# The first MLP product of a decoder layer as seven block products of 256 tokens instead of eight

## The chip, the cores and the metric

The kernel runs on one core of a Trainium2 chip. The metric is the device time of one execution in microseconds (us), the median over runs; a profiled execution is one such run whose instructions were recorded, and its span runs from the first to the last recorded instruction. Engines: PE multiplies matrices (PEld is its loading of weights), DVE, ACT and POOL work elementwise, SP only issues transfers; a transfer (DMA) is issued from the queue of SP, ACT or POOL.

## What is computed

One layer of a decoder on 512 tokens of 1024 features, in float32: a normalised input is projected to gates, queries, keys, values and two short branches; attention, a gated convolution and a pooling are mixed and projected back; then an MLP. The part that matters here:

```
merged = gates[0]*(y_pool @ w_pool_up) + gates[1]*(y_conv @ w_conv_out) + gates[2]*(y_attn @ w_attn_up)
x = x + merged @ w_o                                   # 1024 x 1024
h2 = rms_norm(x, norm_mlp)
x = x + jnp.square(jax.nn.relu(h2 @ w_ff1)) @ w_ff2    # w_ff1: 1024 x 4096, w_ff2: 4096 x 1024
```

The sum of squares inside `rms_norm` is over the features of a token, so its reciprocal root can be multiplied in after `h2 @ w_ff1`, as a factor per token.

## The kernel before

Features lie on the 128 partitions, tokens along the row, so that a tile [128, 512] holds 128 features of all tokens. A weight streams in as units of [128, 1024] (512 KB) by one transfer each on SP's queue; `split` (L115 to L120) cuts it into two float32r parts, `wh` by ACT and `wl` = unit - `wh` by DVE, in buffers of which there are three of each. `mm3` (L122 to L127) makes a float32 product of three passes on PE: `wh` with the high part of the moving tile, `wh` with its low part, `wl` with its high part. One unit feeds 8 x 3 passes of 512 columns.

The order of the work on each engine is fixed when the program is built, by a scheduler that works through the written order; at run time an engine takes its instructions strictly in that order, and each waits for what it reads.

The MLP stage is preceded by the output projection: `wo_mm` (L505) multiplies two of eight merged tiles into four of the eight PSUM banks (a bank is [128, 512]) per unit. `x2_evac` (L555) then adds a bank to the residual `res[m]` (L556) and makes the two parts `xs` of the MLP's input (L164, L167). The first MLP product runs over pairs of output chunks (L581 to L597); `ff1_evac` takes a bank through relu, the factor `rstd2` and the square (L576, L577). `rs2` sums squares of `res` on POOL (`Rstd.add`, L200) and over the partitions by a product with a tile of ones (L204). The second product (L599 on) splits each of its 32 moving tiles (L405, L406) and adds into eight banks.

Of the kernel before, what the change touches and what calls it, by code (L numbers as in the profile page):

```python
# [36 lines left out]
AHEAD = 1  # units of weights split ahead of their use  # L37
WARM = 9  # products of zeros that wake the tensor engine's clock until the first data is there
# [11 lines left out]
def z_order():  # L50
    """The 128-column chunks of w_in, as (kind, index, first column), in the order of use."""
# [14 lines left out]
def hybrid_layer(ctx: ExitStack, tc: tile.TileContext, xT, wst, pmix, vecs, consts, outT):  # L66
# [5 lines left out]
    apool = ctx.enter_context(tc.tile_pool(name="apool", bufs=1))  # L72
# [11 lines left out]
    def tmp(dt=F32):  # L84
        return apool.tile([P, S], dt, tag="tmp", bufs=13, name=nm("tmp"))
# [14 lines left out]
    ahead = deque()  # L100
    rp = None
    n_loaded = [0]

# [3 lines left out]
    def unit():  # L107
        while len(ahead) <= AHEAD and n_loaded[0] < wst.shape[0]:
            raw = raw_unit()
            nc.sync.dma_start(raw, wst[n_loaded[0]])  # L110
            ahead.append(split(raw, rp if n_loaded[0] in LONG else wpool))
            n_loaded[0] += 1
        return ahead.popleft()
# [8 lines left out]
    def mm3(out, w, cols, x, start, stop):  # L122
        """out += w[:, cols].T @ x in float32: both operands split, three float32r passes."""
# [9 lines left out]
    warm = cpool.tile([P, S], BF16, name="warm")  # L133
# [18 lines left out]
    cst = cpool.tile([P, NCONST], F32, name="cst")  # L152
# [6 lines left out]
    bd = cpool.tile([P, P], F32R, name="bd")  # L159
# [10 lines left out]
    def rsqrt_start(total, n):  # L170
        """1 / sqrt(total / n + EPS): by ln and exp, and what then takes one Newton step in float32."""
# [16 lines left out]
    class Rstd:  # L188
        """1 / rms over the features, from their squares as they come in."""
# [44 lines left out]
    # Work that hangs on a chunk of z goes on in steps, one after each later chunk.  # L234
# [12 lines left out]
    at = ExitStack()  # L247
    atp = at.enter_context(tc.tile_pool(name="atp", bufs=1))
# [34 lines left out]
    def v_evac(kind, idx, b):  # L283
# [8 lines left out]
        # [values of one head | ones | values of the other]  # L292
# [101 lines left out]
        # 1 / dn by ln and exp, then one Newton step in float32; dn is at least 1  # L394
# [110 lines left out]
    def wo_mm(half, k, outs):  # L505
        if k % 2 == 0:
            wo_w[half] = unit()
        for i in range(4):
            mm3(outs[i], wo_w[half], cols(4 * (k % 2) + i), merged[k], k == 0, k == KC - 1)

    attn_w = None
    for m in range(KC):
# [10 lines left out]
        if m == 0:  # L523
# [3 lines left out]
            rp = ctx.enter_context(tc.tile_pool(name="rp", bufs=1))  # L527
            for k in range(KC):
# [23 lines left out]
    h2 = [None] * KC  # L552
    rs2 = Rstd()

    def x2_evac(m):  # L555
        nc.vector.tensor_tensor(res[m], res[m], wo_banks[m], OP.add)  # L556
        h2[m] = split_gain(res[m], vec[:, V_NF + m:V_NF + m + 1], True)

    for i in range(4, 8):
        wo_banks[i] = bank()  # L560
    for k in range(KC - 1):
        wo_mm(1, k, wo_banks[4:])
    wo_mm(0, KC - 1, wo_banks[:4])
    for m in range(4):
        x2_evac(m)
    wo_mm(1, KC - 1, wo_banks[4:])
    for m in range(4, 8):
        x2_evac(m)

# [1 line left out]
    f = []  # L571

    def ff1_evac(pair):
        for b in pair:
            t = br(F32) if len(f) < 20 else mg(F32)
            nc.vector.scalar_tensor_tensor(t, b, 0.0, rstd2, op0=OP.max, op1=OP.mult)  # L576
            nc.scalar.activation(t, t, AF.Square)  # L577
            f.append(t)

    done = []  # L580
    for j in range(0, NFF, 2):  # L581
        pair = [bank(), bank()]
        w2 = [unit(), unit()]
        for ks in ([range(4)] + [range(k, k + 1) for k in range(4, KC)] if j == 0 else [range(KC)]):
            for b, w in zip(pair, w2):
                for k in ks:
                    mm3(b, w, cols(k), h2[k], k == 0, k == KC - 1)
        done.append(pair)
        if j == 0:
            for t in res:  # L590
                rs2.add(t)
        if j >= 2:
            if j == 2:
                rstd2 = rs2.end("rstd2")
            for pair in done:
# [109 lines left out]
```

## Time and profile before

| | us |
|---|---|
| median of 3 runs | 824.1 (822.91 to 825.32) |
| span of the profiled execution | 822.6 |
| PE busy | 807.4 (98%) |
| loading of weights (PEld) busy | 662.4 (81%) |
| DVE busy | 424.2 (52%) |
| ACT busy | 297.7 (36%) |
| POOL busy | 63.2 (8%) |

The execution's own time was not recorded beside its span; the median of the runs lies 1.5 us above the span, which is what lies around it. PE is busy almost without a break, and its passes overlap: a pass counts as busy until its last result is out, while the next one has started. How fast PE works is therefore read from the distance between the starts of two passes, not from their durations.

### The profile page before, as it was taken

Reading aid. Unit: us, or ns where it says so; the run is one execution under the profiler, and the core shown is the slowest. Engines: PE = TensorE matmul, PEld = TensorE weight load, DVE = VectorE, ACT = ScalarE, POOL = GpSimd, SP = SyncE. Lnnn points to the kernel's source line nnn. Section 1 sums busy time; section 2 is a strip of 40 time slices with the busy share of each in tenths; the row PEclk is TensorE's granted clock in tenths of the full one; section 3 lists DMA queues with packets and bytes.
Section 4 is the critical chain, followed back from the end, with each engine's and each line's share of the span. In section 5 each row is a group of like instructions: output and inputs, shape, how many; then the busy total and the mean of one; then the engine's idle time right before and its main releaser. Section 6 shows DMA issues by size and latency. Waiting matters only on the chain. (4 is left out here: it accounts for less than half of the span.)

```text
span 822.6 us, 9086 instructions
## 1 busy us (share of the span) xinstructions
PE 807.4 (98%) x3649; PEld 662.4 (81%) x3649; DVE 424.2 (52%) x530; ACT 297.7 (36%) x398; POOL 63.2 (8%) x50
## 2 busy tenths in 40 slices
PE   7999998999999999999999999999999999999998
PEld 4888787887888888888888778888888888888886
DVE  7659686786885434554343756333333333333323
ACT  5466255742363223322232527233223332233210
POOL 6020012124200000000000320000000000000000
PEclk9999999999999999999999999999999999999999
DMA  6422221221254222222222222222222232222312
GB/s 226 154 78 82 97 77 52 90 103 52 77 166 142 100 79 103 103 102 89 91 102 77 73 106 103 96 85 102 103 103 88 91 103 102 99 83 101 102 52 102
DMA packets 24810, 80.99 MB, mean 98 GB/s; under 512 B 2880, under 2 KB 3136, under 8 KB 24768
## 3 DMA queue, kind: packets, MB, share of 16 engines
q1 hardware_dynamic: 23472, 78.19, 27.3%
q10 hardware_dynamic: 1296, 2.23, 0.9%
q8 instruction: 28, 0.46, 0.2%
q14 instruction: 14, 0.11, 0.0%
HBM read 78.31 MB, written 2.10 MB: 98 GB/s over the span
## 5 line engine op out<-in xcount | busy, mean ns | idle before, releaser
L118 ACT ACTIVATE wh<-raw 128x1024 fp32r<-128x1024 f32 x136 | 144.0, 1060 | 406.6 <-issue 212.4
L127 PE MATMUL bank<-xs,wl 128*128 128x512 f32 x720 | 280.7, 390 | 3.6 <-DVE wl L220 2.4
L125 PE MATMUL bank<-xs,wh 128*128 128x512 f32 x720 | 282.0, 393 | 1.8 <-ACT tmp L196 1.8
L126 PE MATMUL bank<-xs,wh 128*128 128x512 f32 x720 | 280.9, 390 | 2.3 <-DVE xs L167 2.2
L119 DVE TENSOR_TENSOR wl<-raw,wh 128x1024 fp32r<-128x1024 f32 x136 | 170.1, 1252 | 68.5 <-ACT wh L118 64.0
L127 PEld LDWEIGHTS bank<-xs,wl 128*128 128x128 f32 x720 | 135.2, 188 | 33.2 <-DVE wl L220 3.4
L126 PEld LDWEIGHTS bank<-xs,wh 128*128 128x128 f32 x720 | 135.2, 188 | 32.9 <-DVE xs L167 4.8
L125 PEld LDWEIGHTS bank<-xs,wh 128*128 128x128 f32 x720 | 135.1, 188 | 31.8 <-ACT tmp L196 2.7
L126 PE MATMUL bank<-tmp,wh 128*128 128x512 f32 x256 | 99.6, 389 | 0.0
L125 PE MATMUL bank<-tmp,wh 128*128 128x512 f32 x256 | 99.6, 389 | 0.0
L127 PE MATMUL bank<-tmp,wl 128*128 128x512 f32 x256 | 99.6, 390 | 0.0
L127 PEld LDWEIGHTS bank<-tmp,wl 128*128 128x128 f32 x256 | 48.0, 188 | 10.2 <-DVE wl L119 0.3
L126 PEld LDWEIGHTS bank<-tmp,wh 128*128 128x128 f32 x256 | 48.1, 188 | 10.0
L125 PEld LDWEIGHTS bank<-tmp,wh 128*128 128x128 f32 x256 | 48.1, 188 | 9.9
L518 DVE TENSOR_TENSOR tmp<-bank,rstd 128x512 f32<-128x512 f32 x24 | 16.6, 692 | 65.5 <-PE bank L127 65.4
L200 POOL TENSOR_TENSOR tmp<-tmp,tmp 128x512 f32<-128x512 f32 x14 | 23.6, 1688 | 247.7 <-ACT tmp L196 246.8
L406 DVE TENSOR_TENSOR tmp<-br,tmp 128x512 fp32r<-128x512 f32 x20 | 13.6, 690 | 44.4 <-PE bank L126 44.4
L576 DVE SCALAR_TENSOR_TENSOR br<-bank,rstd 128x512 f32<-128x512 f32 x20 | 13.5, 689 | 42.9 <-PE bank L127 42.8
L125 PE MATMUL bank<-br,wh 128*128 128x512 f32 x80 | 31.1, 389 | 0.0
L127 PE MATMUL bank<-br,wl 128*128 128x512 f32 x80 | 31.1, 389 | 0.0
L126 PE MATMUL bank<-br,wh 128*128 128x512 f32 x80 | 31.1, 389 | 0.0
L543 DVE TENSOR_TENSOR tmp<-tmp,bank 128x512 f32<-128x512 f32 x24 | 16.5, 688 | 26.0 <-PE bank L127 26.0
(129 smaller groups left out, 671.1 us busy)
## 6 DMA issues: line engine op xcount, KB each, us to landing
raw<-wst SPq DMA_DIRECT2D x136, 512.0 KB, 3.2
raw<-wst SPq DMA_DIRECT2D x8, 256.0 KB, 5.0
mg<-xT SPq DMA_DIRECT2D x8, 256.0 KB, 5.1
res<-xT ACTq DMA_DIRECT2D x8, 256.0 KB, 4.7
outT<-res SPq DMA_DIRECT2D x7, 256.0 KB, 2.0
cst<-consts SPq DMA_DIRECT2D x1, 416.0 KB, 5.4
raw<-pmix SPq DMA_DIRECT2D x1, 256.0 KB, 2.5
outT<-res SPq DMA_DIRECT2D x1, 128.0 KB, 1.8
```

The lines of the kernel that those rows point to most:

```text
L118: nc.scalar.activation(hi, raw, AF.Copy)
L119: nc.vector.tensor_tensor(lo, raw, hi.bitcast(F32), OP.subtract)
L125: nc.tensor.matmul(out, wh[:, cols], xh, start=start, stop=False)
L126: nc.tensor.matmul(out, wh[:, cols], xl, start=False, stop=False)
L127: nc.tensor.matmul(out, wl[:, cols], xh, start=False, stop=stop)
L200: nc.gpsimd.tensor_tensor(self.acc, self.acc, sq, OP.add)
L406: nc.vector.tensor_tensor(lo, t, hi.bitcast(F32), OP.subtract)
L518: nc.vector.tensor_tensor(t, b, rstd, OP.mult)
L543: nc.vector.tensor_tensor(t, t, b, OP.mult)
L576: nc.vector.scalar_tensor_tensor(t, b, 0.0, rstd2, op0=OP.max, op1=OP.mult)
```

## The change

The first MLP product is cut into 2 x 2 blocks (feature halves by column halves of a group of 512 columns of `w_ff1`, and token halves), and the eight block products of a group are replaced by seven, of sums and differences of blocks: P1, P2, Q3, Q4, Q5, Q6, Q7. Each has 8 x 3 passes of 256 columns; there are eight groups. The sums of the moving blocks (`s1` to `s4`, `n22`) are made once by DVE and ACT. The sums of the weight blocks are made by transfers: a block is loaded by SP, split, and after that a transfer on POOL's queue adds the next block onto it in place (`accum_op=OP.add`). So one tile `wx` serves P1, Q5, Q6 and Q4 in turn, with an adding transfer between each two, and one tile `wy` serves Q3 and Q7. The results are put together in `q.f` by DVE and ACT. The second half of the output projection goes by chunks (`wo_chunk`): one bank after the other, all eight merged tiles into it. Pools are placed on the right side of SBUF, so that those of the MLP take the room of the earlier ones tile by tile. Comments were removed.

```diff
+    def wo_chunk(m):
...
+        for k in range(KC):
+            mm3(wo_banks[m], w, cols(k), merged[k], k == 0, k == KC - 1)
...
+    wo_chunk(4)
+    wo_chunk(5)
+    wo_chunk(6)
+    wo_chunk(7)
+    front.close()
...
+    def w1_forms():
+        chain, row = {}, {}
+        for g in range(NFF // 4 + 1):
+            go = g < NFF // 4
+            if go:
+                x = fpool.tile([P, 1024], F32, tag="wx", bufs=3, name=nm("wx"))
+                nc.sync.dma_start(x, w1_block(g, B11))
+                yield "P1", x
+                nc.gpsimd.dma_start(x, w1_block(g, B12), accum_op=OP.add)
+            if g:
+                yield "Q7", row
+            if go:
+                yield "Q5", x
+                nc.gpsimd.dma_start(x, w1_block(g, B22), accum_op=OP.add)
+                z = raw_unit()
+                nc.sync.dma_start(z, w1_block(g, B21))
+                yield "P2", z
+                yield "Q6", x
+                nc.gpsimd.dma_start(x, w1_block(g, B21), accum_op=OP.add)
+            if g:
+                yield "Q4", chain
+            if go:
+                y = fpool.tile([P, 1024], F32, tag="wy", bufs=2, name=nm("wy"))
+                nc.sync.dma_start(y, w1_block(g, B22))
+                yield "Q3", y
+                nc.gpsimd.dma_start(y, w1_block(g, B12), accum_op=OP.add)
+                chain, row = x, y
+
+    forms = w1_forms()
+    ready = deque()
+
+    def w_fill(n):
+        while len(ready) < n:
+            nxt = next(forms, None)
+            if nxt is None:
+                break
+            ready.append((nxt[0], split(nxt[1], wpool)))
+
+    def w_form(kind):
+        w_fill(FORMS_AHEAD + 1)
+        k, w = ready.popleft()
+        assert k == kind, (k, kind)
+        return w
+
...
+    def x2_evac(m):
+        nc.vector.tensor_tensor(res[m], res[m], wo_banks[m], OP.add)
+        nc.scalar.activation(hs[m // 4][:, m % 4], res[m], AF.Copy, scale=vec[:, V_NF + m:V_NF + m + 1])
+
+    a11, a21 = hs[0][:, :, :H], hs[0][:, :, H:]
+    a12, a22 = hs[1][:, :, :H], hs[1][:, :, H:]
...
+    split_form("P1", a11, ALL)
+    w_fill(1)
+    x2_evac(4)
+    x2_evac(5)
+    ks = slice(0, 2)
+    diff(s1, a21, a22, ks)
+    split_form("Q5", s1, ks)
+    split_form("P2", a12, ks)
+    diff(s2, a11, s1, ks)
+    split_form("Q6", s2, ks)
+    for m in range(6):
+        rs2.add(res[m])
+    x2_evac(6)
+    x2_evac(7)
+    ks2 = slice(2, 4)
+    diff(s1, a21, a22, ks2)
+    split_form("Q5", s1, ks2)
+    w_fill(2)
+    split_form("P2", a12, ks2)
+    diff(s2, a11, s1, ks2)
...
+    def product(kind, out, start, stop):
+
+        (wh, wl), (xh, xl) = w_form(kind), sx[kind]
+        for b in range(2):
+            for k in range(4):
...
+                nc.tensor.matmul(o, wh[:, w], xh[:, k], start=first, stop=False, skip_group_check=True)
+                nc.tensor.matmul(o, wh[:, w], xl[:, k], start=False, stop=False, skip_group_check=True)
+                nc.tensor.matmul(o, wl[:, w], xh[:, k], start=False, stop=last, skip_group_check=True)
...
+    for g in range(NFF // 4 + 1):
+        q = None
+        if g < NFF // 4:
+            q = Group()
+            q.A = bank()
+            product("P1", q.A, True, True)
+            q.x1 = tmp()
+            nc.scalar.activation(q.x1, q.A, AF.Copy)
...
+            product("Q7", prev.R, False, True)
+            nc.vector.tensor_tensor(prev.v1, prev.R, prev.x1, OP.subtract)
+            nc.vector.tensor_tensor(prev.f[:, 2:4, H:], halves(prev.v1), halves(prev.x5), OP.add)
...
+            product("Q5", q.T, True, True)
...
+            product("P2", q.A, False, True)
...
+            product("Q6", q.R, True, True)
...
+            product("Q4", prev.R, False, True)
...
+            product("Q3", q.T, False, True)
+            nc.vector.tensor_tensor(q.f[:, 2:4, :H], halves(q.v1), halves(q.T), OP.add)
+        prev = q
```

**Where the change moves instructions.** First place: DVE and ACT where the output projection ends. In the rows `res` is the residual, `bank` a PSUM bank, `wl` and `wh` the parts of a weight, `hs` the MLP's input, `P1l` and the like the parts of a moving block, `s_637` and `s_638` the sums s1 and s2. DVE before, from the sixth residual on:

```order
L556 TENSOR_TENSOR res_2134<-res_2134,bank_3363 128x512
L167 SCALAR_TENSOR_TENSOR xs_3498<-res_2128,vec,xs_3497 128x512
L556 TENSOR_TENSOR res_2136<-res_2136,bank_3364 128x512
L556 TENSOR_TENSOR res_2138<-res_2138,bank_3365 128x512
L167 SCALAR_TENSOR_TENSOR xs_3503<-res_2130,vec,xs_3502 128x512
L119 TENSOR_TENSOR wl_3543<-raw_3540,wh_3542 128x1024
L167 SCALAR_TENSOR_TENSOR xs_3520<-res_2132,vec,xs_3519 128x512
L119 TENSOR_TENSOR wl_3549<-raw_3546,wh_3548 128x1024
L167 SCALAR_TENSOR_TENSOR xs_3525<-res_2134,vec,xs_3524 128x512
```

DVE of the change, from the seventh residual on:

```order
L650 TENSOR_TENSOR res_2142<-res_2142,bank_3448 128x512
L650 TENSOR_TENSOR res_2144<-res_2144,bank_3473 128x512
L665 TENSOR_TENSOR P1l<-hs_3507,P1h 128x1024
L129 TENSOR_TENSOR wl_3529<-wx_3526,wh_3528 128x1024
L670 TENSOR_TENSOR s_637_3509<-hs_3507,hs_3508 128x512
L665 TENSOR_TENSOR P2l<-hs_3508,P2h 128x512
L670 TENSOR_TENSOR s_638_3510<-hs_3507,s_637_3509 128x512
L665 TENSOR_TENSOR Q5l<-s_637_3509,Q5h 128x512
L665 TENSOR_TENSOR Q6l<-s_638_3510,Q6h 128x512
L670 TENSOR_TENSOR s_637_3509<-hs_3507,hs_3508 128x512
L670 TENSOR_TENSOR s_638_3510<-hs_3507,s_637_3509 128x512
L129 TENSOR_TENSOR wl_3576<-wx_3526,wh_3575 128x1024
```

ACT of the change, over the same stretch (L206 squares a residual, L128 makes `wh`, `tmp_3616` is the copy of P1's bank, `raw_3586` the weights of P2):

```order
L206 ACTIVATE tmp_3558<-res_2136 128x512
L664 ACTIVATE Q6h<-s_638_3510 128x512
L206 ACTIVATE tmp_3561<-res_2138 128x512
L206 ACTIVATE tmp_3564<-res_2140 128x512
L651 ACTIVATE hs_3508<-res_2142,vec 128x512
L651 ACTIVATE hs_3508<-res_2144,vec 128x512
L128 ACTIVATE wh_3575<-wx_3526 128x1024
L664 ACTIVATE Q5h<-s_637_3509 128x512
L664 ACTIVATE P2h<-hs_3508 128x512
L664 ACTIVATE Q6h<-s_638_3510 128x512
L128 ACTIVATE wh_3588<-raw_3586 128x1024
L729 ACTIVATE tmp_3616<-bank_3584 128x512
```

Before, the parts of a residual tile follow it and the weights of the first pair lie between; now P1's own parts stand behind the last residual, and on ACT the weights of Q5 (`wh_3575`) and then of P2 and the copy of P1's bank stand behind squares and splits that hang on DVE.

Second place: POOL and PE around the sum of squares. POOL before and of the change (L200 and L210 add squares, L610, L615, L620 and L627 are the adding transfers):

```order
L200 TENSOR_TENSOR tmp_3600<-tmp_3600,tmp_3602 128x512
L200 TENSOR_TENSOR tmp_3600<-tmp_3600,tmp_3605 128x512
L200 TENSOR_TENSOR tmp_3600<-tmp_3600,tmp_3608 128x512
L200 TENSOR_TENSOR tmp_3600<-tmp_3600,tmp_3611 128x512
L200 TENSOR_TENSOR tmp_3600<-tmp_3600,tmp_3614 128x512
L200 TENSOR_TENSOR tmp_3600<-tmp_3600,tmp_3617 128x512
L200 TENSOR_TENSOR tmp_3600<-tmp_3600,tmp_3620 128x512
```

```order
L610 DMA wx_3526<-wst 128x1024
L210 ISA
L210 TENSOR_TENSOR tmp_3550<-tmp_3550,tmp_3552 128x512
L615 DMA wx_3526<-wst 128x1024
L210 TENSOR_TENSOR tmp_3550<-tmp_3550,tmp_3555 128x512
L210 TENSOR_TENSOR tmp_3550<-tmp_3550,tmp_3558 128x512
L210 TENSOR_TENSOR tmp_3550<-tmp_3550,tmp_3561 128x512
L210 TENSOR_TENSOR tmp_3550<-tmp_3550,tmp_3564 128x512
L210 TENSOR_TENSOR tmp_3550<-tmp_3550,tmp_3623 128x512
L210 TENSOR_TENSOR tmp_3550<-tmp_3550,tmp_3626 128x512
L620 DMA wx_3526<-wst 128x1024
```

PE before and of the change, around the product with ones:

```order
L125 MATMUL bank_3624<-xs_3534,wh_3627 128x512
L126 MATMUL bank_3624<-xs_3535,wh_3627 128x512
L127 MATMUL bank_3624<-xs_3534,wl_3628 128x512
L204 MATMUL bank_3685<-tmp_3600,ones 128x512
L125 MATMUL bank_3709<-xs_3487,wh_3633 128x512
L126 MATMUL bank_3709<-xs_3488,wh_3633 128x512
```

```order
L705 MATMUL bank_3584<-P2h,wh_3588 128x256
L706 MATMUL bank_3584<-P2l,wh_3588 128x256
L707 MATMUL bank_3584<-P2h,wl_3589 128x256
L214 MATMUL bank_3629<-tmp_3550,ones 128x512
L705 MATMUL bank_3641<-Q5h,wh_3575 128x256
L706 MATMUL bank_3641<-Q5l,wh_3575 128x256
L707 MATMUL bank_3641<-Q5h,wl_3576 128x256
```

The six later additions of squares now stand behind the second adding transfer (L615), which waits for the split of Q5's weights, and the product with ones stands ahead of all of Q5.

Third place: DVE of the change in one later group, from the split of Q7's weights to that of Q3's and the subtraction behind it (L742, L744, L716, L757 and L770 put results together); before there are two splits and two evacuations (L576) for a pair of chunks:

```order
L129 TENSOR_TENSOR wl_4201<-wy_4133,wh_4200 128x1024
L770 TENSOR_TENSOR f_4130<-tmp_4163,bank_4070 128x2x256
L129 TENSOR_TENSOR wl_4231<-wx_4166,wh_4230 128x1024
L129 TENSOR_TENSOR wl_4264<-raw_4261,wh_4263 128x1024
L741 TENSOR_TENSOR tmp_4163<-bank_4132,tmp_4033 128x512
L742 TENSOR_TENSOR f_4130<-tmp_4163,tmp_4099 128x2x256
L129 TENSOR_TENSOR wl_4297<-wx_4166,wh_4296 128x1024
L744 SCALAR_TENSOR_TENSOR f_4130<-f_4130,rstd_3631 128x1024
L129 TENSOR_TENSOR wl_4328<-wx_3941,wh_4327 128x1024
L716 SCALAR_TENSOR_TENSOR f_4355<-bank_4229,rstd_3631 128x2x256
L129 TENSOR_TENSOR wl_4361<-wy_4358,wh_4360 128x1024
L757 TENSOR_TENSOR tmp_4388<-bank_4357,tmp_4258 128x512
```

From one `wy` to the next all seven splits of a group stand in one line with the evacuations.

## Rows read from the trace of the kernel before

**Rows 1.** Page, busy time of each engine, share, instructions.

```profile
PE 807.4 (98%) x3649; PEld 662.4 (81%) x3649; DVE 424.2 (52%) x530; ACT 297.7 (36%) x398; POOL 63.2 (8%) x50
```

**Rows 2.** Windows: first MLP product; length, PE, PEld, DVE, ACT, POOL, PEclk, DMA, GB/s.

```profile
464.95:644.42 179.47, 176.49 (x771) 144.22 (x770) 77.41 (x82) 65.27 (x88) 12.08 (x7) 1.00 0.28 97
```

**Rows 3.** Timeline of PE, end of the first product: start, duration, instruction.

```profile
638.53 0.39 PE L126 MATMUL bank<-xs,wh 128*128 128x512 f32 x1
...
643.97 0.39 PE L126 MATMUL bank<-xs,wh 128*128 128x512 f32 x1
```

**Rows 4.** Timeline of PE in attention: pairs of float32 passes of 128 columns.

```profile
119.52 0.39 PE L380 MATMUL bank<-br,vx 128*128 128x128 f32 x2
...
121.75 0.39 PE L387 MATMUL bank<-br,vx 128*128 128x128 f32 x2
```

**Rows 5.** Weight loads of such passes: ns min/median/max, first and last start.

```profile
L389 PEld LDWEIGHTS bank<-br,vx x32: 192/192/333, 121.0 to 236.2; 128*128 128x128 f32 x32
```

**Rows 6.** Timeline of PE: the product with ones, two float32 passes of 512 columns.

```profile
491.19 1.02 PE L204 MATMUL bank<-tmp,ones 128*128 128x512 f32 x2
```

**Rows 7.** Page, transfers: SP's queue, and issues with KB and us to landing.

```profile
q1 hardware_dynamic: 23472, 78.19, 27.3%
...
raw<-wst SPq DMA_DIRECT2D x136, 512.0 KB, 3.2
...
cst<-consts SPq DMA_DIRECT2D x1, 416.0 KB, 5.4
```

**Rows 8.** DVE by line and form: count, busy us, mean ns, idle before.

```profile
L119 DVE TENSOR_TENSOR wl<-raw,wh 128x1024 fp32r<-128x1024 f32 x77 | 96.4, 1253 | 52.2 <-ACT wh L118 48.1 <-PE bank L204 4.2
L406 DVE TENSOR_TENSOR tmp<-br,tmp 128x512 fp32r<-128x512 f32 x20 | 13.6, 690 | 44.4 <-PE bank L126 44.4
L576 DVE SCALAR_TENSOR_TENSOR br<-bank,rstd 128x512 f32<-128x512 f32 x20 | 13.5, 689 | 42.9 <-PE bank L127 42.8
L556 DVE TENSOR_TENSOR res<-res,bank 128x512 f32<-128x512 f32 x8 | 5.3, 683 | 1.3 <-PE bank L127 1.3
```

**Rows 9.** ACT by line and form.

```profile
L118 ACT ACTIVATE wh<-raw 128x1024 fp32r<-128x1024 f32 x136 | 144.0, 1060 | 406.6 <-issue 212.4 <-PE bank L126 188.4 <-DVE xs L166 3.4
L577 ACT ACTIVATE br<-br 128x512 f32<-128x512 f32 x20 | 12.1, 617 | 1.1 <-DVE br L576 1.1
L173 ACT ACTIVATE tmp<-bank,epst 128x512 f32<-128x512 f32 x14 | 9.4, 674 | 2.8 <-PE bank L204 2.7
L175 ACT ACTIVATE tmp<-tmp 128x512 f32<-128x512 f32 x14 | 8.8, 631 | 0.4
L164 ACT ACTIVATE xs<-res,vec 128x512 fp32r<-128x512 f32 x8 | 5.6, 715 | 3.3 <-DVE res L556 3.3
L175 ACT ACT_TABLE_LOAD x1 | 1.3, 1283 | 0.0
```

**Rows 10.** Timeline of ACT: two squares back to back.

```profile
467.05 1.14 ACT L196 ACTIVATE tmp<-res 128x512 f32<-128x512 f32 x2
```

**Rows 11.** POOL by line and form.

```profile
L200 POOL TENSOR_TENSOR tmp<-tmp,tmp 128x512 f32<-128x512 f32 x14 | 23.6, 1688 | 247.7 <-ACT tmp L196 246.8
```

**Rows 12.** Timeline of DVE around the end of the output projection.

```profile
460.39 2.05 DVE L556 TENSOR_TENSOR res<-res,bank 128x512 f32<-128x512 f32 x3 [1.31 <-PE bank L127]
...
468.45 2.31 DVE L119 TENSOR_TENSOR wl<-raw,wh 128x1024 fp32r<-128x1024 f32 x1
```

**Rows 13.** Timeline of PE there: a wait.

```profile
470.81 0.50 PE L127 MATMUL bank<-xs,wl 128*128 128x512 f32 x1 [1.25 <-DVE wl L119]
```

**Rows 14.** Timeline of POOL there: six additions of squares.

```profile
466.20 11.30 POOL L200 TENSOR_TENSOR tmp<-tmp,tmp 128x512 f32<-128x512 f32 x6
```

**Rows 15.** Timeline of PE in attention: a wait.

```profile
130.90 0.49 PE L379 MATMUL bank<-br,vx 128*128 128x128 f32 x2 [2.14 <-ACT br L370]
```

**Rows 16.** Window of 3.4 us behind that wait, columns as in rows 2.

```profile
131.70:135.10 3.40, 3.21 (x15) 3.21 (x16) 2.42 (x4) 3.28 (x6) 0.08 (x1) 0.51 0.02 5
```

More of the change, by code (lines that the diff above doesn't have):

```diff
@@ L37 @@
 AHEAD = 1
+FORMS_AHEAD = 2
 WARM = 9
@@ L100, in hybrid_layer @@
     ahead = deque()
-    rp = None
+    lp = None
     n_loaded = [0]
+    end = [wst.shape[0] - 2 * NFF]
     def raw_unit():
@@ L107, in unit @@
     def unit():
-        while len(ahead) <= AHEAD and n_loaded[0] < wst.shape[0]:
+        while len(ahead) <= AHEAD and n_loaded[0] < end[0]:
             raw = raw_unit()
             nc.sync.dma_start(raw, wst[n_loaded[0]])
-            ahead.append(split(raw, rp if n_loaded[0] in LONG else wpool))
+            ahead.append(split(raw, lp if n_loaded[0] in LONG else wpool))
             n_loaded[0] += 1
@@ new lines, in hybrid_layer, with w1_block @@
+    B11, B12, B22, B21 = range(4)
+    def w1_block(g, i):
+        return wst[base + 4 * g + i]
+    def w1_forms():
[25 more added lines that the diff above has]
+                chain, row = x, y
@@ L559, in hybrid_layer, with diff_tile, split_form @@
[L559 to L563, printed above, removed]
+        nc.scalar.activation(hs[m // 4][:, m % 4], res[m], AF.Copy, scale=vec[:, V_NF + m:V_NF + m + 1])
+    a11, a21 = hs[0][:, :, :H], hs[0][:, :, H:]
+    a12, a22 = hs[1][:, :, :H], hs[1][:, :, H:]
+    sx = {}
+    def diff_tile(name):
+        return ftile(name)[:, 0:2].rearrange("p a (b c) -> p (a b) c", c=H)
+    def split_form(kind, t, ks):
+        if kind not in sx:
+            sx[kind] = [spool.tile([P, 4, H], F32R, name=f"{kind}{part}") for part in "hl"]
+        hi, lo = (x[:, ks] for x in sx[kind])
+        nc.scalar.activation(hi, t[:, ks], AF.Copy)
+        nc.vector.tensor_tensor(lo, t[:, ks], hi.bitcast(F32), OP.subtract)
@@ L564, in hybrid_layer, with diff @@
+    s1, s2, s4, s3, n22 = (diff_tile(n) for n in ("s1", "s2", "s4", "s3", "n22"))
+    def diff(t, a, b, ks):
+        nc.vector.tensor_tensor(t[:, ks], a[:, ks], b[:, ks], OP.subtract)
+    ALL = slice(0, 4)
     for m in range(4):
         x2_evac(m)
-    wo_mm(1, KC - 1, wo_banks[4:])
-    for m in range(4, 8):
-        x2_evac(m)
-    f = []
[L573 to L595, printed above, removed]
-                ff1_evac(pair)
-            done = []
+    split_form("P1", a11, ALL)
@@ new lines, in hybrid_layer @@
+    w_fill(1)
[17 more added lines that the diff above has]
+    diff(s2, a11, s1, ks2)
+    split_form("Q6", s2, ks2)
+    def product(kind, out, start, stop):
+        (wh, wl), (xh, xl) = w_form(kind), sx[kind]
+        for b in range(2):
+            for k in range(4):
+                w = cols(4 * b + k)
+                first, last = start and b == 0 and k == 0, stop and b == 1 and k == 3
+                o = out[:, b * H:(b + 1) * H]
+                nc.tensor.matmul(o, wh[:, w], xh[:, k], start=first, stop=False, skip_group_check=True)
+                nc.tensor.matmul(o, wh[:, w], xl[:, k], start=False, stop=False, skip_group_check=True)
+                nc.tensor.matmul(o, wl[:, w], xh[:, k], start=False, stop=last, skip_group_check=True)
@@ L599, in hybrid_layer @@
+    n_loaded[0] = base + NFF
+    end[0] = wst.shape[0]
+    sm.close()
+    opool = right(back, "opool", reuse_waits="tile")
+    tmps[:] = [opool, 10]
     outs = [bank() for _ in range(8)]
@@ L614, in hybrid_layer @@
             eng.dma_start(outT[:, m, t], res[m][:, t])
+    back.close()
 def _chunk(w, c):
```

89 lines of the change are left out of this document (74 added, 15 removed).

## Prediction

> **What bounds the kernel now.** The page first: PE is busy 98% of the span, DVE 52%, ACT 36% and POOL 8% [rows 1]. The windows then give the stage that is rewritten: the first MLP product lasts from 464.95 to 644.42, 179.5 us, with PE busy in 176.5 and DVE and ACT less than half [rows 2]. The timeline of PE gives the pace inside: 24 passes of 512 columns from 638.53 to 643.97, 0.2267 us each [rows 3]. The stage has 32 chunks x 8 x 3 = 768 passes, 174.1 us; the other 5.4 us are the product with ones (0.86) [rows 6] and waits at the start, of which one is for the low part of a weight that DVE made while POOL added squares [rows 12 to 14]. So PE's passes end last, and what counts is how many, how far apart, and what they wait for.
>
> **Passes: fewer columns.** Seven products x 24 passes x 8 groups = 1344 passes of 256 columns. No row has such a pass. Bounds for the distance between two: a quarter of the 0.43 us that one float32 pass of 512 columns took (1.02 less the other's start, two passes 0.86), if columns alone count, 0.1075 [rows 6]; the same 0.1075 plus all that a pass of 512 now has above two of these, 0.2267 - 0.2150, 0.119; and the nearest row, float32 passes of 128 columns, which stream as long and load new weights each time: 20 from 119.52 to 121.75, 0.1115 [rows 4]. I take half of 0.2267, 0.1134: 152.4 us, 2.72 a product (144.5 and 159.9 at the bounds). On PE alone the change takes off 21.7 us.
>
> Each pass still loads its own weights. Loads of 192 ns each stood in those attention passes and started as often as the passes, every 0.11 us [rows 4, 5], so they overlap each other and I charge nothing. Perfetto Trace Analysis in the Trainium skill (Identifying the Most-Contended Engine) takes the busy share of weight loading as the better measure of headroom. By that rule the loads, 0.187 us each now (144.22 over 770) [rows 2], would need 1344 x 0.187 = 251 us, more than the whole stage has; the rows of attention speak against that.
>
> **The start of the MLP, worked out by its order.** Time runs from the end of the last output chunk. A split or sum takes 1.25 us on DVE for 1024 elements and 0.69 for 512 [rows 8], 1.06 and 0.62 on ACT [rows 9], or 0.57 back to back [rows 10]; hand-overs between engines are put at 0.05 to 0.1.
> - DVE adds the last residual (0.68) and only then makes P1's low half and P1's low weights: 3.3. Before, PE waited here too, for 1.25 [rows 13]. P1 ends at 5.9.
> - The first adding transfer (L610) may start at 3.3, since it overwrites what DVE just read. With a time D from issue to landing, it lands at 3.3 + D.
> - ACT stands at a split that needs s1 (4.0); with seven more instructions behind it at 0.57 each, 8.6. Then come Q5's high weights (9.6), three splits, P2's high weights and the copy of P1's bank, without which P2 may not add into it: 13. DVE makes Q5's low weights at 11.2 and, behind three splits, P2's at 14.5. PE idles from 5.9 to about 14.
> - POOL starts the second adding transfer at 11.2 and only then the six later additions: 1.69 us each over the kernel [rows 11], but 11.3 for six at this very place [rows 14]: 22.5. PE has the product with ones ahead of Q5: 23.5.
> - Q5 and Q6 run to 29.2. Q3 waits for a copy that ACT makes behind the root's chain, 0.67 + 0.63 + 0.63 + 0.63 and two table loads of 1.28 [rows 9], Q3's own weights and the copy, 6.8 in all: 30.2. P1 of the next group starts at 32.9 and not at 13.6.
>
> **Steady groups.** PE needs 7 x 2.72 = 19.05. DVE has 7 x 1.25 for weights and some 6 of evacuations, ACT 7 x 1.06 and some 3, so neither is the bound by its sum. But one line closes on itself: the split of Q7's weights is followed by a sum (0.69) and Q5's low weights (1.25); then B22 is added (D), Q6 is split (1.06 + 1.25), an evacuation of 1024 (put at 1.25), Q4's weights (1.25), an evacuation (0.69) and Q3's weights (1.25) follow, the other block is added (D), and Q7 is split again (1.06 + 1.25). That is 11.0 + 2D and some 0.5 of hand-overs. It stays under 19.05 only while D is below 3.8.
>
> **D, which no row shows.** From below: a plain load of 512 KB from SP lands 3.2 after its issue [rows 7]. Of that the moving is 1.5, since 78.19 MB held the 16 engines for 27.3% of 822.6 us. From above: an add has to fetch what stands there as well, so twice the load, 6.4; loads that met a full queue at the kernel's start took 5.4 for 416 KB. I take the 1.7 of fixed time and two movings, 4.7, and 0.3 for other transfers: a group then has three loads and four adds, 16.5 us of transfers' time in some 21, where the stage now has a share of 0.28 [rows 2]. D = 5.0, a group 21.5.
>
> **Sum.** To the second P1 32.9; the first full group 19.05 + 4.6 (Q7's moving block is split by ACT and DVE only after its weights, which land at 35.2: it starts at 39.7 where PE was free at 35.6, and Q6 waits 0.5), 56.6; six groups of 21.5, 185.6; the last Q7 and Q4, 5.4, with 5.1 of waits, since no P1 stands between; then 3.7 until the second MLP product, because ACT makes its first moving part behind a weight split that waits for Q4's end and two squares (1.06 x 3 + 0.62): 199.8. That is 20.3 more than the 179.5. The clock: after a wait of 2.1 us in attention it was granted at 0.51 for 3.4 us, the lower of its two levels, 1.2 instead of 2.4 GHz [rows 15, 16]. The start has longer waits; where passes are the bound behind them, from 23.5 on, 3.4 us at half pace cost 1.7. Span 822.6 + 20.3 + 1.7 = 844.6, and 1.5 as before between span and median: **846 us**. The output projection has as many passes as before and is charged nothing; the 24 more loads and adds in all are priced in D.
>
> **Rivals.**
> - **An add costs no more than a load** (D = 3.2). Then groups are PE's, 19.05: 32.9, 54.3, 168.6, and 10.7 behind, 179.3 and the same stage time as before: 825.6 with the clock. For it: only the transfer's latency differs. Against it: twice the bytes to fetch. The Trainium skill's DMA: Bandwidth & Descriptors (Anatomy of one DMA) gives a transfer issued by POOL 2.0 us and its bytes at 436 GB/s, an estimate of 3.2 for a plain one; by it the sum would be this rival's. No run here shows a transfer of POOL.
> - **Faster: cheap adds and passes bound by columns alone.** At 0.1075 a product takes 2.58 and a group 18.06, and 46 products behind the start save 0.14 each, 6.5, with 0.7 in the start: 818. It decides below D = 3.3 and a distance of 0.112. For it: the product with ones ran at that rate. Against it: passes of 512 have 0.0117 above it.
> - **Slower than forecast: adds queue behind one another** and D is 6.6 or more. The line gives 2 us a group for each us of D, 14.5 in all: from 870 on. For it: waits of 5 us in full queues; and two-input work of DVE took 2.31 instead of 1.25 while POOL worked [rows 12], which would do the same if POOL is busy writing out its transfers. Against it: never more than two adds are open.
> - **Weight loads one after another.** 770 of them were busy for 144.22 us, 0.187 each [rows 2]; if none overlaps the next, 1344 take 251 us and with the start's waits the time is over 900. Against it stand the loads in attention.
>
> **How the numbers follow.** The forecast, D from 3.6 to 6.6 (830 to 870), has 0.65; an add at a load's price 0.16 (820 to 830); faster 0.08; queued adds 0.09; loads in a row 0.02. The range leaves out the faster case and the last two: 824 to 870. 0.3% are 2.5 us, about what a measurement of this kernel can tell from no change: faster 0.10 (the third case and some of the second), the same 0.08, slower 0.82.
>
> **What would show it.** Right: passes of 256 columns 0.11 to 0.12 apart; PE idle about 2 + 8 + 6 us around P1, P2 and the product with ones; P1's starts 21 to 22 us apart later on, with Q7 and Q6 waiting for weights that wait for an adding transfer; the clock at its lower level once in the start. The sum is wrong if adds land in under 3.8 us, if POOL starts later additions while a transfer of its queue still waits, or if the distance of passes is above 0.13, which makes PE the bound of every group.

## The result, and the profile after

The changed kernel takes 884.15 us (median of 4 runs, 882.38 to 886.4), the kernel before 824.36 beside it: 1.0721 times as long, 95% interval 1.0698 to 1.0744. The forecast was 846 us (824 to 870): slower it is, by 60 us and not by 22. The profiled execution, the slowest of the four, took 886.4 us with a span of 884.6, against a forecast span of 844.6.

From the page of the changed kernel: busy time of the engines, PE and its granted clock in 40 slices, the two queues that load weights, and the issues with KB and us to landing (before: [rows 1, 7]).

```profile
PE 824.7 (93%) x4225; PEld 695.8 (79%) x4225; DVE 477.5 (54%) x594; ACT 334.9 (38%) x433; POOL 90.1 (10%) x82
...
PE   7999999999999999999994788988888799999998
...
PEclk9999999999999999999998799999999799999999
...
q1 hardware_dynamic: 22320, 74.00, 24.5%
q0 software_dynamic: 4608, 16.78, 11.4%
...
wx<-wst POOLq DMA_DIRECT2D x24, 512.0 KB, 5.8
...
wy<-wst POOLq DMA_DIRECT2D x8, 512.0 KB, 6.6
```

Before, PE was busy 98% of the span. The holes are in the slices of the first MLP product, and the windows say how much each stretch of it took. They are the front, the first group up to the second P1, five steady groups (P1 of the third to P1 of the eighth), the last group up to the second MLP product, and that product; columns as in [rows 2].

```profile
0.00:471.02 471.02, 463.83 (x2111) 376.32 (x2112) 283.79 (x382) 189.52 (x259) 51.01 (x43) 0.99 0.31 105
471.02:509.54 38.52, 20.51 (x123) 18.49 (x122) 22.52 (x24) 19.29 (x27) 15.34 (x12) 0.73 0.33 59
534.99:662.12 127.13, 109.38 (x842) 104.80 (x841) 69.54 (x75) 49.92 (x55) 17.25 (x20) 0.96 0.66 141
662.12:701.84 39.72, 30.25 (x219) 28.71 (x217) 23.07 (x26) 17.47 (x20) 2.59 (x3) 0.90 0.45 99
701.84:884.60 182.76, 178.99 (x768) 146.11 (x768) 60.41 (x70) 46.87 (x60) 0.00 (x0) 0.98 0.27 90
```

The stage lasts 701.84 - 471.02 = 230.8 us; it was 179.5 [rows 2], and 199.8 was forecast. The excess of 40 us over the forecast span is made of six pieces: the front 6.1 (471.02 against 464.95, forecast 0), the first group 5.6 (38.5, forecast 32.9), the second 1.8 (25.45, forecast 23.65), the five steady groups 19.6 (25.43 each, forecast 21.5), the end 4.0 (39.7 against 35.7), and the second MLP product 4.6 (182.8; before 822.6 - 644.4 = 178.2); less the 1.7 that the forecast had for the clock.

One steady group, in the timelines of POOL (issues) and of ACT (splits that wait for a transfer): start, length, instruction, and the wait with what ended it.

```profile
581.19 0.86 POOL L627 DMA_DIRECT2D wy<-wst  x1 [3.57 <-DVE wl L129]
582.93 0.86 POOL L610 DMA_DIRECT2D wx<-wst  x1 [0.87 <-DVE wl L129]
594.09 0.86 POOL L615 DMA_DIRECT2D wx<-wst  x1 [10.30 <-DVE wl L129]
602.61 0.86 POOL L620 DMA_DIRECT2D wx<-wst  x1 [7.65 <-DVE wl L129]
607.04 0.86 POOL L627 DMA_DIRECT2D wy<-wst  x1 [3.58 <-DVE wl L129]
608.78 0.86 POOL L610 DMA_DIRECT2D wx<-wst  x1 [0.87 <-DVE wl L129]
```

```profile
588.25 1.06 ACT L128 ACTIVATE wh<-wy 128x1024 fp32r<-128x1024 f32 x1 [7.67 <-DMA wy<-wst]
...
591.48 1.06 ACT L128 ACTIVATE wh<-wx 128x1024 fp32r<-128x1024 f32 x1 [1.22 <-DMA wx<-wst]
...
600.00 2.01 ACT L128 ACTIVATE wh<-wx 128x1024 fp32r<-128x1024 f32 x2 [6.03 <-DMA wx<-wst]
```

This is the loop of the forecast with one link changed. L610 goes out at 582.93 and Q5's block can be split at 591.48: 8.55. The split and POOL's answer take until 594.09, 2.61. L615's transfer is there at 600.00: 5.91. Splits and evacuations take 8.78 until the next L610 at 608.78. Together 25.85, of which 11.39 are not transfers (forecast 11.5), and 14.46 are two transfers (forecast 10.0). POOL itself writes at each issue for 0.86, and L610 stands 1.74 behind L627, so that two adding transfers are open at once.

The changed link: the forecast's line had L627 here, the transfer onto `wy` for Q7. That one takes 7.06 (581.19 to 588.25), and Q7's split and sum follow. But Q5's block is then not there yet: ACT stands idle for 1.22 more, until L610 has landed. So the line over L627 comes to 24.6 for this group, and L610, which goes out behind the split of P1's weights and which the line left out, sets the 25.85.

The start, in the timelines of PE (waits), of ACT, and of POOL:

```profile
487.26 0.58 PE L705 MATMUL bank<-P2h,wh 128*128 128x256 f32 x1 [10.16 <-ACT tmp L729]
...
497.42 2.07 PE L214 MATMUL bank<-tmp,ones 128*128 128x512 f32 x2 [5.31 <-POOL tmp L210]
498.50 1.20 PE L705 MATMUL bank<-Q5h,wh 128*128 128x256 f32 x1
499.50 0.41 PE L706 MATMUL bank<-Q5l,wh 128*128 128x256 f32 x1
```

```profile
486.61 0.60 ACT L729 ACTIVATE tmp<-bank 128x512 f32<-128x512 f32 x1 [2.85 <-POOL tmp L210]
```

```profile
121.80 1.45 POOL L279 TENSOR_TENSOR tmp<-tmp,tmp 128x512 fp32r<-128x512 f32 x1 [7.43 <-issue]
129.10 1.80 POOL L371 PARTITION_ALL_REDUCE tmp<-tmp  x1 [5.86 <-issue]
...
474.51 1.18 POOL L610 DMA_DIRECT2D wx<-wst  x1 [246.13 <-DVE wl L129]
484.91 1.67 POOL L210 TENSOR_TENSOR tmp<-tmp,tmp 128x512 f32<-128x512 f32 x1 [9.22 <-issue]
486.53 1.05 POOL L615 DMA_DIRECT2D wx<-wst  x1
487.32 10.04 POOL L210 TENSOR_TENSOR tmp<-tmp,tmp 128x512 f32<-128x512 f32 x6
```

The waits are where the forecast had them, for P2 and the product with ones. P2's is 10.16 and not some 8: ACT's copy of P1's bank stood 2.85 for POOL's next addition. And POOL stood still for 9.22 us between its first adding transfer and its next addition, with nothing to wait for that the profile shows. The rows at 121.80 and 129.10 show such gaps where POOL goes from its all-reduce (L371) to additions, 7.43, and back, 5.86. The last all-reduce is at 226.60, 248 us earlier, but POOL's order, as the program was built, has the change back to additions (an ISA row of L210) behind the first transfer; from the changed kernel:

```
L371 ISA tmp_1839<-tmp_1833 128x512
L610 DMA wx_3526<-wst 128x1024
L210 ISA
L210 TENSOR_TENSOR tmp_3550<-tmp_3550,tmp_3552 128x512
L615 DMA wx_3526<-wst 128x1024
```

The Trainium skill's GPSIMD Engine Reference (2.1 Instruction dispatch) tells of some 6 us for the first call of a freshly loaded routine of POOL, which no instruction in a profile shows. Of the gaps of this trace the one of 5.86 agrees; 7.43 and 9.22 are longer.

### The profile page after: what moved, and what is told of

Its sections match the earlier page's. It is cut to its first block, busy times and chain, and to the rows that moved or that the text cites. A ratio compares the mean times of both kernels' runs of the same rounds, so it can differ in the third digit from the quotient of the medians.

```text
span 884.6 us, 10405 instructions
## 1 busy us (share of the span) xinstructions
PE 824.7 (93%) x4225; PEld 695.8 (79%) x4225; DVE 477.5 (54%) x594; ACT 334.9 (38%) x433; POOL 90.1 (10%) x82
## 3 DMA queue, kind: packets, MB, share of 16 engines
q0 software_dynamic: 4608, 16.78, 11.4%
## 5 line engine op out<-in xcount | busy, mean ns | idle before, releaser
L128 ACT ACTIVATE wh<-raw 128x1024 fp32r<-128x1024 f32 x112 | 118.4, 1057 | 302.9 <-PE bank L136 170.7
L129 DVE TENSOR_TENSOR wl<-raw,wh 128x1024 fp32r<-128x1024 f32 x112 | 138.6, 1238 | 131.2 <-ACT wh L128 130.9
L137 PE MATMUL bank<-xs,wl 128*128 128x512 f32 x464 | 183.1, 395 | 2.6 <-DVE wl L230 2.6
L135 PE MATMUL bank<-xs,wh 128*128 128x512 f32 x464 | 184.2, 398 | 0.6 <-ACT tmp L206 0.6
L136 PE MATMUL bank<-xs,wh 128*128 128x512 f32 x464 | 183.7, 396 | 0.6 <-DVE xs L177 0.6
L137 PEld LDWEIGHTS bank<-xs,wl 128*128 128x128 f32 x464 | 88.0, 190 | 22.9 <-DVE wl L230 3.6
L135 PEld LDWEIGHTS bank<-xs,wh 128*128 128x128 f32 x464 | 87.9, 190 | 22.5 <-ACT tmp L206 1.0
L136 PEld LDWEIGHTS bank<-xs,wh 128*128 128x128 f32 x464 | 87.9, 189 | 20.2 <-DVE xs L177 1.3
L129 DVE TENSOR_TENSOR wl<-wx,wh 128x1024 fp32r<-128x1024 f32 x32 | 40.2, 1255 | 39.2 <-ACT wh L128 39.2
L136 PEld LDWEIGHTS bank<-tmp,wh 128*128 128x128 f32 x256 | 48.8, 190 | 11.5
L128 ACT ACTIVATE wh<-wx 128x1024 fp32r<-128x1024 f32 x32 | 33.1, 1053 | 54.2 <-DMA wx<-wst 50.6
L129 DVE TENSOR_TENSOR wl<-wy,wh 128x1024 fp32r<-128x1024 f32 x16 | 19.6, 1224 | 43.0 <-ACT wh L128 43.0
L128 ACT ACTIVATE wh<-wy 128x1024 fp32r<-128x1024 f32 x16 | 16.8, 1050 | 53.0 <-DMA wy<-wst 53.0
L610 POOL DMA_DIRECT2D wx<-wst x8 | 7.2, 902 | 253.7 <-DVE wl L129 253.7
```

Of the source, the lines that this page charges most:

```text
L128: nc.scalar.activation(hi, raw, AF.Copy)
L129: nc.vector.tensor_tensor(lo, raw, hi.bitcast(F32), OP.subtract)
L135: nc.tensor.matmul(out, wh[:, cols], xh, start=start, stop=False)
L136: nc.tensor.matmul(out, wh[:, cols], xl, start=False, stop=False)
L137: nc.tensor.matmul(out, wl[:, cols], xh, start=False, stop=stop)
L610: nc.gpsimd.dma_start(x, w1_block(g, B12), accum_op=OP.add)
```

## The experiments

Times are medians; the ratio is that to the kernel before, run beside it on the same chip, with its 95% interval.

| run | us | ratio | interval |
|---|---|---|---|
| the change | 884.15 | 1.0721 | 1.0698 to 1.0744 |
| e1_chunks_alone | 821.28 | 0.9956 | 0.9941 to 0.9972 |
| e2_chunks_and_pools | 828.17 | 1.0045 | 1.0029 to 1.0061 |
| e3_plain_on_pool | 850.62 | 1.0313 | 1.0285 to 1.0341 |
| e4_plain_on_sp | 835.13 | 1.0130 | 1.0115 to 1.0146 |
| e5_tiles_shifted | 880.17 | 1.0685 | 1.0649 to 1.0721 |
| e6_links_apart | 843.71 | 1.0228 | 1.0198 to 1.0258 |
| e7_filled_waits | 884.47 | 1.0749 | 1.0692 to 1.0806 |
| e8_apart_and_shifted | 842.76 | 1.0213 | 1.0183 to 1.0244 |
| e9_early_squares | 877.57 | 1.0624 | 1.0594 to 1.0655 |
| e10_all_together | 838.10 | 1.0149 | 1.0123 to 1.0176 |
| e11_together_no_overlap | 837.47 | 1.0145 | 1.0114 to 1.0176 |
| e12_apart_early_squares | 841.09 | 1.0196 | 1.0164 to 1.0228 |

### Is it the adding transfers?

```diff
-                nc.gpsimd.dma_start(x, w1_block(g, B12), accum_op=OP.add)
+                nc.gpsimd.dma_start(x, w1_block(g, B12))     # e3; all four
+                nc.sync.dma_start(x, w1_block(g, B12))       # e4; all four
```

> The changed kernel with each adding transfer as a plain one on the same queue (weight sums left out). Loop theory: a group is 11.5 us of splits and evacuations and two transfers that are waited for, which took 5.9 to 8.5 us from issue to landing. Plain ones should land in about 4.1 (0.86 of issue, 3.2), the loop falls to 19.7, PE's seven products at 0.118 a pass take 19.8: P1 starts 20 to 20.5 us apart instead of 25.4, and the time is 840 to 848. Rival, contention or PE itself: P1 starts stay above 24 apart, over 875. Rival, the queue of POOL costs as much as the adding: landing stays above 5.5, groups above 23, over 865.

> The same with plain transfers issued by SP (weight sums left out). Loop theory: landing in 3.2 to 3.5, groups at PE's 20, 840 to 846, within 4 us of the plain ones on POOL. If POOL's queue were the cost, this is far below that run. If neither the queue nor the adding matters, groups stay at 25 and the time above 875.

Steady groups in windows of e3 (three groups) and of e4 (four), and the queue and issues of e3:

```profile
548.14:609.01 60.87, 60.62 (x507) 59.74 (x505) 41.50 (x45) 29.62 (x33) 6.36 (x12) 1.00 0.55 181
```

```profile
541.86:621.01 79.15, 79.15 (x675) 79.15 (x674) 58.06 (x61) 42.29 (x46) 0.00 (x0) 1.00 0.55 182
```

```profile
q0 software_dynamic: 4608, 16.78, 6.1%
...
wx<-wst POOLq DMA_DIRECT2D x24, 512.0 KB, 4.1
...
wy<-wst POOLq DMA_DIRECT2D x8, 512.0 KB, 4.6
```

With plain transfers the groups are 20.3 and 19.8 us, PE is busy in all of it in e4, and the waits are gone: the loop theory holds. What held the groups was the adding; POOL's queue as such costs some 0.5 a group. The same bytes held the 16 engines for 11.4% of 884.6 us when added, 3.15 each over 32 transfers, and for 6.1% of 844.9 when only copied, 1.61. e3 is a few us above its range, e4 below: the start still has POOL's standstill in e3 (37.1 us to the second P1), and not in e4 (31.8), which has no transfer of POOL. So the expectation that the two lie within 4 us failed: they are 15.5 apart. In the profiles e4's stage is 16.2 shorter, 5.3 of it at the start, 3.6 in the second group, 2.3 in the steady ones and 5.1 at the end.

### The same adding transfers, further apart

```diff
-  P1(g) Q7(g-1) Q5(g) P2(g) Q6(g) Q4(g-1) Q3(g)
+  P1(g) Q6(g-1) P2(g) Q7(g-1) Q5(g) Q4(g-1) Q3(g)
```

The lines are the order in short. The residuals, splits and sums at the start of the MLP were put in another order to suit it.

> The changed kernel with its products in another order (P1 of a group, then Q6 of the one before, P2, Q7, Q5, Q4, Q3), so that each adding transfer has three products between the form before it and the one after it instead of one; same products, same transfers. The product with ones moves behind Q6. Loop theory: landing still 5.8 or more, but P1 starts 20 us apart in steady groups, with no waits in them; the MLP's start falls by 10 or more; 828 to 842. Rival, bandwidth or POOL's queue: 32 transfers hold the groups as before, 24 or more apart, over 870.

Four steady groups in a window of e6, and its issues:

```profile
544.27:623.42 79.15, 79.15 (x674) 79.15 (x673) 57.13 (x60) 41.60 (x44) 13.84 (x16) 1.00 0.84 181
```

```profile
wx<-wst POOLq DMA_DIRECT2D x24, 512.0 KB, 5.5
...
wy<-wst POOLq DMA_DIRECT2D x8, 512.0 KB, 5.4
```

All 32 adding transfers are there, and groups are 19.79 us with no wait. So the transfers cost nothing in steady groups when three other products lie between a form and the next one made from it, though all transfers together fill more of the 16 engines' time there than in the changed kernel (0.84 against 0.66). An adding transfer that goes out 5 us or more behind the one before takes 5.4 in the median of these groups (L629, L622), one 2.5 behind 5.6 (L610), against 8.55 for the one 1.74 behind in the changed kernel. The time is 1.7 above what was expected, because of the start: to the fourth P1 it is 74.8 us (544.27 - 469.45; before this edit 89.7), where three groups at 19.8 need 59.4. Too few products stand there that need no sum.

### The clock

```diff
+    def fill(n):
+        b = bank()
+        for _ in range(n):
+            nc.tensor.matmul(b[:, :H], sx["P1"][0][:, 0, :P], sx["P1"][0][:, 0], start=True, stop=True)
...
+            if g > 1:
+                fill(FILL)                                    # FILL = 10
             product("Q7", prev.R, False, True)
```

The same ahead of Q6; the added passes write a bank that nothing reads.

> The changed kernel with 10 extra passes of 256 columns into an unused bank ahead of Q7 and of Q6 from the second group on (1.2 us of each wait of 2.6). Clock theory: windows at the lower clock between 520 and 700 go (there were five of 3.4 and they seemed to cost some 2 us each), groups are 24 us apart throughout: 872 to 878. Rival, the windows are hidden by the loop: within 2 us of 884. If the extra passes lengthen the loop, 890 or more.

```profile
534.01:661.28 127.27, 116.87 (x943) 113.39 (x941) 69.39 (x75) 49.84 (x55) 17.30 (x20) 0.99 0.66 140
```

The granted clock in the five steady groups rose from 0.96 to 0.99 and they took as long as before, 127.27 against 127.13. The rival is right: in steady groups the lower clock is hidden by the loop.

### The pace of the passes

```diff
 # e1: the kernel before, with
-    for k in range(KC - 1):
-        wo_mm(1, k, wo_banks[4:])
...
     for m in range(4, 8):
+        wo_chunk(m)
         x2_evac(m)
 # e2: the changed kernel with the first MLP product of before, in the pools of the change
 # e5: the changed kernel with
+    zpool.tile([P, FRONT_PAD], F32, name="padz")              # FRONT_PAD = 80
-    warm = zpool.tile([P, S], BF16, name="warm")
+    warm = tmp().bitcast(BF16)[:, :S]
+    bpad.tile([P, BACK_PAD], F32, name="padb")                # BACK_PAD = 272
```

> The kernel before with one part of the change: the second half of the output projection by chunks, residuals added as chunks end; pools and the MLP stay as before. The first MLP product started 6 us later after the change (471.0 against 464.95). If the order by chunks made that, this run is 5 to 7 us slower than before, 829 or so. If it is the pace (passes of 512 were 0.2288 apart after the change, 0.2267 before, from the first chunk on), and the pace comes from something else, this run keeps 0.2267 and is within 3 us of before.

> The changed kernel with the first MLP product of before (eight plain block products' worth, passes of 512 columns): chunks, and the pools where the change put them. If the place of the tiles sets the pace, passes of 512 are 0.2288 apart here too, 3400 of them cost 7 us: 830 to 833. If the pace comes with the new product, they are 0.2267 apart and the time is 823 to 826, some of it for residuals that are all added at the end.

> The changed kernel, with its tiles moved and nothing else: in front the moving tiles stand a multiple of 1024 bytes from the weight tiles, in the MLP a multiple of 2048, as they did before the change (there 0 modulo 2048; after it 320 and 1088). If this distance sets the pace, passes of 512 are 0.2267 apart again instead of 0.2288 (2600 of them, 5.4 us) and passes of 256 about 0.1135 instead of 0.118; the groups' loop hides most of the second: 876 to 880. If the distance does not matter, 0.2288, 0.118 and 882 to 886.

> Both the other order of products and the shifted tiles. If the pace follows the tiles' distance, passes of 256 at 0.1135 make a group 19.1 and this run is 10 to 12 us below the one with the other order alone, 817 to 830; if not, the same as that one.

Passes of the front in the timeline of PE, of e1, e2 and e5: in each the first row and the 85th, 84 distances on.

```profile
299.81 0.39 PE L126 MATMUL bank<-xs,wh 128*128 128x512 f32 x1
...
318.86 0.39 PE L126 MATMUL bank<-xs,wh 128*128 128x512 f32 x1
```

```profile
299.81 0.39 PE L136 MATMUL bank<-xs,wh 128*128 128x512 f32 x1
...
319.02 0.39 PE L136 MATMUL bank<-xs,wh 128*128 128x512 f32 x1
```

```profile
299.75 0.39 PE L140 MATMUL bank<-xs,wl 128*128 128x512 f32 x1
...
318.79 0.39 PE L140 MATMUL bank<-xs,wl 128*128 128x512 f32 x1
```

That is 19.05, 19.21 and 19.04 us, or 0.2268, 0.2287 and 0.2267 a pass. e1 and e2 have the same chunks and the same first MLP product and differ by 6.9 us: 3360 passes by 0.0021 are 7.1. e2 itself lies 2 us under its range, as the chunks gain 3 (e1). So the place of the tiles sets this pace, and shifting them gave it back. For passes of 256 the expectation failed: 0.118 became 0.120 in e5 and e8, and in e10 too, where the distance was 1024, so that the distance in bytes does not explain them. e5 lies 4 us under the changed kernel and e8 1 under e6, which the spread of the runs hardly tells apart, instead of 5.4 and 10 to 12. Besides the passes of 256, the shift has a price at the start: P1 begins 4.2 us after the start of the last chunk's last pass in e5 and e8, and 0.2 after it in the changed kernel and e6. ACT in e5, the first scaled residuals:

```profile
462.86 3.17 ACT L656 ACTIVATE hs<-res,vec 128x512 f32<-128x512 f32 x5 [14.08 <-PE bank L140]
```

They wait 14.08 for passes of the output projection; no such wait stands in the changed kernel or e6.

e1 is also a result: chunks alone are 0.44% faster than before. The wait of [rows 13] is gone, since the last chunk works on while the residuals of the ones before it are split.

### The start

```diff
     for m in range(4):
         x2_evac(m)
+        rs2.add(res[m])
...
-    for m in range(6):
-        rs2.add(res[m])
```

> The changed kernel with the squares of each residual added as soon as the residual is there, so that four of POOL's additions, and the change of its configuration ahead of them, come before its first adding transfer. In the changed kernel that change stood behind the transfer and the next addition began 9.2 us after it. If this is what made the start 5.6 us longer than forecast, the second adding transfer goes out 4 us earlier, the product with ones waits for nothing, and the second P1 comes 31 to 34 us after the first instead of 38.5: 877 to 880. Rival, the start hangs on the split behind the first adding transfer alone: second P1 still 37 or more after the first, 882 to 886.

POOL in e9:

```profile
461.85 1.29 POOL L210 TENSOR_TENSOR tmp<-tmp,tmp 128x512 f32<-128x512 f32 x1 [1.90 <-ACT tmp L206]
472.70 1.18 POOL L610 DMA_DIRECT2D wx<-wst  x1 [9.55 <-issue]
473.62 1.60 POOL L210 TENSOR_TENSOR tmp<-tmp,tmp 128x512 f32<-128x512 f32 x1
```

The standstill behind L610 is gone, the second P1 comes 32.2 us after the first (501.10 - 468.93), and the time falls as expected. But the second adding transfer goes out 13.5 after P1's start where it was 15.5, so 2 earlier and not 4, and the product with ones begins after 18.6 where it was 26.4. e9 moves the additions with the change of configuration, so how much of the 6.3 us each of the two gave is not shown.

The last three put the pieces together: e10 has P1 and P2 of two groups ahead of the first form that needs a sum, then pairs of groups (P1a P2a Q7y Q4y P1b Q5a P2b Q3a Q5b Q6a Q3b Q7a Q6b Q4a, y the group before), early squares and shifted tiles; e11 shifts the MLP's tiles further; e12 is e8 with early squares.

> Links four products apart in pairs of groups, P1 and P2 of two groups ahead of the first form that needs an adding transfer, early squares, and tiles shifted so that passes of 512 run at 0.2267; same products and transfers. If waits, POOL's order and pace are all that the changed kernel lost, the first MLP product takes 3.3 + 56 x 2.83 + some 8 of waits at both ends = 170 to 175 instead of 230.8, and the time is 814 to 822, under before (824). If the lower clock after the start's waits or the end of the stage still costs 5 or more: 823 to 832. Distance of tiles in the MLP here is 1024 bytes: passes of 256 at 0.118 or less if 0 was the worse place.

> The run with all together, with the MLP's tiles shifted by 1088 bytes instead of 64. There the first scaled residual waited 14 us for tiles of the front that stood in its place, and the first P1 began 5.3 us late. If the place alone made that, P1 starts within 1 us of the last chunk's end and the time is 831 to 835, still above before (824), since DVE's splits and sums hold the start. If the whole remaining loss were that wait and its lower clock, 822 to 828.

> Links apart in the order of one group at a time, tiles shifted, and the squares added early. Against the same without the early squares (842.8): POOL's configuration no longer stands behind the first adding transfer, so the second one goes out some 4 us earlier and the start is 4 to 7 us shorter, 835 to 839. If the start hangs on DVE's splits alone, the same 841 to 844.

ACT in e11, the first scaled residual:

```profile
464.01 0.73 ACT L657 ACTIVATE hs<-res,vec 128x512 f32<-128x512 f32 x1 [14.08 <-PE bank L140]
```

All three stay above the kernel before. e10 misses both of its ranges: its stage takes 184.1 us and not 170 to 175, and begins late. That wait stands in e10, e11 and e12 as in e5 and e8, and P1 begins more than 5 us after the last chunk in e10 to e12; so the expectation that the MLP's shift makes it fell, and e11 misses its ranges too. All five runs with shifted tiles have the wait, and e5 has nothing but the shift, so the shift makes it. Its part in front is left, and was not tried alone. e12 lies 1.7 us under e8, not 4 to 7, and their runs overlap. Its rival, the splits on DVE, fits the row of POOL's second adding transfer, which goes out no earlier after P1 than in e8 (14.9 and 14.8 us):

```profile
486.32 0.88 POOL L627 DMA_DIRECT2D wx<-wst  x1 [4.80 <-DVE wl L132]
```

## Why the forecast was right in its sign and wrong in its size

- **Passes.** Forecast 0.1134, measured 0.118 in steady groups (Q6 of e6: 24 in 2.83), inside the bounds, and 0.120 with shifted tiles, just above them. 56 products of 24 passes make it 6 us of PE's time, which the loop hid in the changed kernel and e6 shows: 19.8 a group, not 19.05. Weight loads overlap, as argued: in e6's window of 79.15 us stand 673 loads of some 0.188 each, 127 us. The rule of Perfetto Trace Analysis in the Trainium skill, by which the busy share of weight loading tells the headroom, would have given 251 us here. The trace does not agree: the stage has 230.8, and the same passes took 19.8 a group in e6, 158 for eight.
- **The loop** was right in kind: its splits and evacuations, put at 11.5, come to 11.7 on the forecast's line in the group shown (24.6 less 7.06 and 5.91), and to 11.39 on the line that ends last. **Here the step failed: D = 5.0.** Over the five steady groups L615 took 5.9 in the mean, 0.9 more, and L627 7.0, 2.0 more. The third part, 1.0 a group, is ACT's wait for L610, which the line left out. Together that is the 3.9 by which a group is over 21.5.
- **Why D was too small.** The estimate had a fixed time and two movings, 4.7. The two movings were right (3.15 against 1.61 in e3). It left out that POOL writes each transfer for 0.86, where SP takes 0.33; an adding transfer that no other is close ahead of takes 5.4 (e6). And it dismissed the third rival, adds that queue behind one another, because never more than two are open. Two are enough: L627 and L610 go out 1.7 to 2.2 apart in the steady groups, and in the one shown they take 7.06 and 8.55. By the forecast's own price, 14.5 us for each us of D, 2.0 more, for (25.43 - 11.39) / 2 = 7.0 on the line that ends last, are 29 us; the second group, the five steady ones and the end are 25.4 over the forecast.
- **The start** was sized at 32.9 and took 38.5. The step that failed is POOL's, as the forecast put it: "POOL starts the second adding transfer at 11.2 and only then the six later additions: 22.5". It stood still for 9.22 behind its first transfer, so the second went out at 15.5, and Q5 began at 27.5 instead of 23.5. The ISA row was there to be read; it has no duration in any view, and I passed over it. Q5 then ran mostly at the lower clock, 498.50 to 503.76 (granted 0.57), 2.5 us more than 2.72; Q3's forecast wait of 1.0 fell away. 4.0 + 2.5 - 1.0 = 5.5. e9, without the standstill and with the additions early, has 32.2; e4, which has no transfer of POOL ahead of the change, 31.8.
- **The clock** was priced at 1.7. In the start it cost the 2.5 just told, in Q7 of the last group some 2.8 of the end's time (24 passes 0.2335 apart), and some 2.9 at the head of the second MLP product (granted 0.53 from 701.84 to 708.20); in steady groups nothing (e7).
- **"The output projection is charged nothing"** was right of the chunks, which gain (e1), and wrong of the pools that came with them: 0.0021 on each of 2604 passes of 512 outside the stage, 5.5 of the 10.7 us that the front and the second MLP product took longer. The rest is some 2.4 us in the kernel's first 25, which e2 and e3 with the same front have not, and the head of the second MLP product, which ran at the lower clock.
- **An add at a load's price** fell: in the changed kernel adds take 5.8 and 6.6 in the median (`wx`, `wy`) where plain transfers on the same queue take 4.1 and 4.6 (e3). The Trainium skill's DMA: Bandwidth & Descriptors (Anatomy of one DMA) comes out at an estimate of 3.2 for a plain transfer of POOL; the shortest in e3 take 3.4.

Left open: why passes of 256 columns are 0.118 apart in most stretches and 0.1135 in two of the changed kernel (503 to 512 and 617 to 619); how much of the start's 6.3 us in e9 is the standstill and how much the earlier additions; and which part of the shift makes the first scaled residuals wait.

## What to carry to other kernels

Where a value is changed in place by a transfer and used between two changes, the time of a group can be the sum of a loop and not the busiest engine: write down every such loop, and price each transfer with its issue on the engine that writes it and with the one ahead of it in the queue. Moving the uses apart can then hide the transfers as they are (e6: 40 us; plain transfers on the same queue, e3, 34). A change that saves PE's time by products with longer preparation pays at its start: here the passes save 15.7 us (174.1 - 8 x 19.8), and no run with the seven products came under the kernel before: start and end took more.

## What the runs showed of the hardware

- An adding transfer of 512 KB holds the 16 engines for 3.15 us, a plain one for 1.61, and occupies POOL for 0.86 instead of 0.53 (e3). With another 1.74 ahead of it, it landed after 8.55, with one 2.5 ahead after 5.6 in the median (e6).
- POOL stood for 5.86 before an all-reduce that followed additions, and for 7.43 and 9.22 before additions that followed an all-reduce. The last of these stood where the change has its place in POOL's order, behind L610, after 246 us of idling; in e9, where the change stands ahead of L610, there is nothing behind it.
- The place of the tiles changed the distance of passes of 512 columns by 0.9% (0.2267 and 0.2288).
- At the lower clock passes of 256 columns were 0.213 apart, and at the full one 0.1135 to 0.120. In the first group the granted clock was 0.73 on average, after waits of 10.16 and 5.31 us.
